# First feed-forward product: the third pair's first four block products ahead of the last ones of the first two pairs, and the sums of the first results spread over later products

## The chip, the cores and the metric

The kernel runs on one core of one Trainium2 chip, in one launch. The metric is the time of an execution on the device in microseconds (us).

## The reference

A decoder block on x (1, 1024, 1024), float32: two token mixers side by side, a gated merge, then a feed-forward part, with adaptive norms in front of both and a norm at the end. The change lies in the first product of the feed-forward part:

```python
h = modulate(rms_norm(x, norm2_g[l]), sh2, sc2)
x = x + g2[:, None, :] * squared_relu_mlp(h, w_ff1[l], w_ff2[l])

def squared_relu_mlp(h, w1, w2):
    return jnp.square(jax.nn.relu(h @ w1)) @ w2     # w1 1024 x 4096, w2 4096 x 1024
```

## The kernel before

Everything is transposed: features lie on the 128 partitions, the 1024 tokens on the free axis. Every float32 operand of a matmul is split into a high half (rounded by ScalarE, a cast) and a low half (VectorE, the operand less the high half), and each product is three matmuls: low times high, high times low, high times high (`mm3`, lines 219, 221, 223).

**Pairs and seven products.** The first feed-forward product makes 4096 hidden features in 16 *pairs* of 128-feature tiles, pair 0 to pair 15 (the first pair is pair 0). Each pair is computed by a Strassen-like scheme: weights and activations are cut into 2 x 2 blocks, and seven block products replace eight. Their names, in the order of a pair, are `ORDER = ("11", "s1", "s3", "s2", "12", "22", "s4")`. A product is twelve matmuls of 128 x 128 by 128 x 512: four slices of the inner dimension by the three of `mm3`. (2,"s3") below means product "s3" of pair 2.

Products work on operands made from the activations: "11" and "12" on blocks of the activations, "s1", "s2", "s3" and "22" on sums of blocks (t1, t2, t3, t4), "s4" on a block. On the weights' side "s1" to "s4" use sums of weight blocks: a running sum that each of the "s" products of a pair takes on from the one before ("s3" has a buffer half of its own).

**PSUM banks.** Each pair has four banks, and some products share one: "11" and "12" bank 0 (called a), "s1" and "s4" bank 1 (d), "s2" bank 2 (b), "s3" and "22" bank 3 (c). The second product of a bank adds to what the first one left.

**The class `Blocks`** records the work of a pair:

- `prep` makes the weights of a product ready: for an "s" product VectorE adds two blocks (line 261); ScalarE casts the high half (line 266). The low half (line 276) is put off until the next `prep`, or `flush`, so that VectorE need not wait for the cast at once.
- `mm` records the twelve matmuls.
- `post` works on the results. After "11" ScalarE copies a (line 298). After "s2" VectorE does the combining: u less b (line 309), then v = c less u (line 310), then the output of "22" from v and d (line 2220). After "12", "22" and "s4" three more outputs follow. The first two pairs use another form, in which d is copied out of PSUM first (lines 302, 305, 306).
- Each output goes through relu and square on ScalarE (lines 2221, 2222 or 2218, 2222) and is stored by a DMA of SP's queue (lines 2228, 2230).
- `run` walks a list of products. For each it calls `before` (loads), records the matmuls, prepares the weights of later products as slots come free, does `post` and calls `after`.

**Slots.** Prepared weights live in 18 slots. Some of them (one tag for a first use, later the ring of six tiles `wh` and `wl` and two of the pool `att`) are used again, so that `run` prepares about as many products ahead as it has finished.

**Sums for the second product.** The second feed-forward product needs sums of blocks of the hidden activations. `a_sums(q, 0)` makes two of them (lines 2237, 2238), `a_sums(q, 1)` two more (lines 2241, 2242), each pair of sums in one tile, stored by one DMA (line 2244).

**The order of work.** Nothing is reordered behind the program: each engine runs its instructions in the order in which they were recorded, and waits on semaphores. `ff1` writes the beginning out by hand: the products of pairs 0 and 1 alternate, while VectorE and ScalarE still make the operands t1 to t4 out of the second half of the tokens. Then `run` takes over with the rest, beginning with

```python
items = sums[:2] + [(0, "22"), (1, "22")] + sums[2:]
late = {(0, "22"): (0, 0), (1, "22"): (1, 0), (2, "s2"): (0, 1), (2, "12"): (1, 1)}
```

so that the order on TensorE is (2,"11"), (2,"s1"), (0,"22"), (1,"22"), (2,"s3"), (2,"s2"), (2,"12"), (2,"22"), (2,"s4"), (3,"11") and so on. `late` says after which product which sums are made.

**Weights from HBM.** `w1_load(q, part)` loads the two halves of a pair's weights on SP's queue (line 2194): pair 2 into the ring `raw` of three tiles, from pair 3 on into the ring `g0` of eight, which also holds the outputs. SP's queue works in order too: a load behind a store waits until that store's data are ready.

Of the kernel before, what the change touches and what calls it, by code (L numbers as in the profile page):

```python
# [133 lines left out]
def block_kernel(ctx, tc, io, stop=None, dbg=None):  # L134
# [240 lines left out]
    def rstd_rows(acc, name, pool, meanwhile=None):  # L375


        nb = acc.shape[1] // P
        ss = ps_s(name + "ss")
        for b in range(nb):  # L380
            nc.tensor.matmul(ss[:, b:b + 1], acc[:, b * P:(b + 1) * P], ones, start=True, stop=True)
        if meanwhile:
            meanwhile()
        return rstd_of(ss[:, :nb], name, pool)
# [8 lines left out]
    def rstd_bcast(rs, b0, nb, name):  # L393

        rb = ps_s(name + "rb")
        for b in range(nb):
            nc.tensor.matmul(rb[:, b * P:(b + 1) * P], rs[:, b0 + b:b0 + b + 1].to_broadcast([P, P]),
                             ident, start=True, stop=True)
        return rb[:, :nb * P]
# [1701 lines left out]
    def x1_load(f, src=None):  # L2101

        t = G["p"].tile([P, S], F32, tag="g0", bufs=8, name=f"x1{'r' if src else ''}_{f}")
        nc.sync.dma_start(t, (src or io["xT"])[f])
        G["x1", f] = t
# [77 lines left out]
    NS = 3  # L2183
    a_d = {t: dram.tile([P, S], F32, name=f"ad{t}") for t in range(8 * NS, 2 * NQ)}
    xs_d = [dram.tile([P, 7, 4, 512], F32, name=f"xsd{c}") for c in range(NS)]
    def w1_load(q, part):

        if q < 2:
            t = G["p"].tile([P, 1024], F32, tag="g1", bufs=8, name=f"w1r{q}{part}")
        elif q < 3:  # L2190
            t = wraw.tile([P, 1024], F32, tag="raw", name=f"w1r{q}{part}")
        else:
            t = G["p"].tile([P, 1024], F32, tag="g0", bufs=8, name=f"w1r{q}{part}")
        nc.sync.dma_start(t, io["w_ff1"][2 * q + part - 1])
        BF.raw[q, part] = t
# [36 lines left out]
    def a_sums(q, part):  # L2232

        e, o = M["out", q]
        r = A["r1"].tile([P, 2, 512], F32, tag="att", bufs=8, name=f"as{q}{part}")
        if part == 0:
            nc.vector.tensor_sub(r[:, 0], e[:, :512], e[:, 512:])
            nc.vector.scalar_tensor_tensor(r[:, 1], r[:, 0], -1.0, o[:, 512:], op0=ALU.mult, op1=ALU.subtract)
            M["t2", q] = r[:, 1]
        else:  # L2240
            nc.vector.tensor_sub(r[:, 0], o[:, 512:], e[:, 512:])
            nc.vector.scalar_tensor_tensor(r[:, 1], M.pop(("t2", q)), -1.0, o[:, :512], op0=ALU.mult,
                                           op1=ALU.subtract)
        nc.sync.dma_start(xs_d[q // 4][:, 3 + 2 * part:5 + 2 * part, q % 4], r)

    BF = Blocks("f", X, ["g1"] * 4 + ["att*"] * 4 + ["att"] * 2 + ["att*"] * 2 + ["wh", "wl"] * 3,
                lambda kind: kind in ("att", "wh", "wl"), f_place, f_sums, f_temps, f_out)

    def x_split(name, m, src, pool, tag, bufs, k=None):

        if tag == "mh":
            hi, lo = mh(f"x{name}{m}h"), mh(f"x{name}{m}l")
        else:
            t = pool.tile([P, 1024], F32R, tag=tag, bufs=bufs, name=f"x{name}{m}")
            hi, lo = t[:, :512], t[:, 512:]
        X[name, m] = hi, lo
        if k is None:
            nc.scalar.copy(hi, src)
            return lambda: nc.vector.tensor_sub(lo, src, fv(hi))
        sh = mods[:, SH2 + k:SH2 + k + 1]  # L2260
        nc.scalar.activation(hi, src, AF.Identity, bias=sh)
        return lambda: nc.vector.scalar_tensor_tensor(lo, src, sh, fv(hi), op0=ALU.add, op1=ALU.subtract)

    def ff1(ahead):
        def t_(k, half):
            return G["x1", k][:, 512 * half:512 * half + 512]

        def norm(k):
            t = t_(k, 1)
            nc.vector.scalar_tensor_tensor(t, t, a2[:, k:k + 1], G["rb"], op0=ALU.mult, op1=ALU.mult)  # L2270


        BF.mm(0, "11", range(3))
        G["rs"] = rstd_rows(G["acc", "n21"], "n21", G["mp"], lambda: BF.prep((2, "11"), (2, "s1")))
        BF.mm(0, "11", range(3, 4))
        BF.post(0, "11")
        BF.mm(1, "11", range(2))
        G["rb"] = rstd_bcast(G["rs"], 0, 4, "n21")
        BF.mm(1, "11", range(2, 4))
        BF.post(1, "11")  # L2280
        BF.prep((2, "s3"))
        BF.mm(0, "12")
        BF.mm(1, "12")
        low = None
        for m in range(4):
            norm(2 * m)
            t1 = t_(2 * m, 0)
            nc.vector.tensor_sub(t1, t1, t_(2 * m, 1))
            if low:
                low()  # L2290
            low = x_split("t1", m, t1, None, "mh", 32)
        norm(1)
        low()
        BF.mm(0, "s1")
        BF.mm(1, "s1")
        for m in range(4):
            if m > 0:
                norm(2 * m + 1)
                low()
            low = x_split("22", m, t_(2 * m + 1, 1), None, "mh", 32, 2 * m + 1)  # L2300
            if m % 2 == 0:
                BF.post(m // 2, "s1")
        for m in range(4):
            t3 = t_(2 * m, 1)
            nc.vector.scalar_tensor_tensor(t3, t3, dsh[:, m:m + 1], t_(2 * m + 1, 1), op0=ALU.add, op1=ALU.subtract)
            low()
            if m == 0:
                BF.mm(0, "s4")
                BF.mm(1, "s4")
            low = x_split("t3", m, t3, G["p"], "g1", 8)  # L2310
        for m in range(4):
            k = 2 * m + 1
            t = t_(k, 1)
            nc.vector.scalar_tensor_tensor(t, t, mods[:, SH2 + k:SH2 + k + 1], t_(2 * m, 0), op0=ALU.add, op1=ALU.add)
            low()
            if m == 0:
                BF.mm(0, "s3")
                BF.mm(1, "s3")
            low = x_split("t2", m, t, G["p"], "g1", 8)

        def t4(m):
            k = 2 * m + 1
            t = t_(k, 0)
            nc.vector.scalar_tensor_tensor(t, t, mods[:, SH2 + k:SH2 + k + 1], t_(k, 1), op0=ALU.add, op1=ALU.subtract)
            return x_split("t4", m, t, A["r1"], "att", 8)

        l = t4(0)
        low()
        BF.mm(0, "s2")
        BF.mm(1, "s2")  # L2330
        BF.post(0, "s2")
        l()
        low = t4(1)
        l = t4(2)
        low()
        BF.post(0, "12")
        BF.post(1, "s2")
        l()
        low = t4(3)
        BF.post(0, "s4")  # L2340
        low()
        BF.post(1, "12")
        BF.post(1, "s4")
        for k in range(NK):
            del G["x1", k]
        for part in (1, 2):
            w1_load(3, part)
        sums = [(q, n) for q in range(2, NQ) for n in ORDER]
        items = sums[:2] + [(0, "22"), (1, "22")] + sums[2:]

        def before(q, n):
            if (q, n) == (2, "22"):
                for part in (1, 2):
                    w1_load(4, part)
            if q > 2 and n == ORDER[0] and q + 2 < NQ:
                for part in (1, 2):
                    w1_load(q + 2, part)
            if q == NQ - 1 and n in ("s2", "12"):
                for f in range(3):
                    x1_load(f + 3 * (n == "12"), x1_d)  # L2360

        late = {(0, "22"): (0, 0), (1, "22"): (1, 0), (2, "s2"): (0, 1), (2, "12"): (1, 1)}
        late.update({(q + 1, n): (q, part) for q in range(2, 4 * NS) for part, n in enumerate(("11", "s1"))})

        def after(q, n):
            if (q, n) in late:
                a_sums(*late[q, n])
            if q == NQ - 2 and n in ("12", "22"):
                b_raw(0, "11", int(n == "22"))
            if q == NQ - 1:  # L2370
                second_ahead(n)

        BF.run(items, sums[3:], before, after, ("s2",))
        x1_load(6, x1_d)
        x1_load(7, x1_d)
        b_x(1, 0)
        b_x(1, 1)
# [17 lines left out]
    def b_raw(c, b, s):  # L2395

        tag = RAWS[c][b].split()[s]
        pool = {"raw": wraw, "rl": G["mp"]}.get(tag, whl)
        t = pool.tile([P, 1024], F32, tag=tag, bufs=2 if tag == "rl" else 3, name=f"w2r{c}{b}{s}")
        nc.sync.dma_start(t, io["w_ff2s"][(4 * c + ("11", "12", "21", "22").index(b)) * 2 + s])  # L2400
        B[c, b, s] = t
# [213 lines left out]

    nff = DFF // P
    steps.add(ff1, manual=True)
    steps.add(ff2_blocks, manual=True)
    behind = []
# [146 lines left out]
```

## Time and profile before

| | us |
|---|---|
| three runs | 2184.2, 2184.3, 2186.07 |
| median | 2184.3 |
| the profiled execution | 2182.82 |
| its span, first to last instruction | 2181.1 |
| 1.7 us lie around the span | |

The mean granted clock of TensorE in the profiled execution is 0.998 of full speed. The first feed-forward product runs from 1534 us to 1849 us of the span.

How to read the views: PE is TensorE (matmuls), PEld its weight loads, DVE VectorE, ACT ScalarE, SP the engine whose queue issues the DMAs. A row of a timeline has start, duration, engine, source line, operation, output<-inputs, shape; in brackets the idle time in front of it and what ended it. A matmul's row lasts 0.39 us, but matmuls overlap: one starts every 0.23 us. A row of the waits has the waiting engine, tile and line, the one waited for, the total in us, how many times, the longest. A row of the stretches has its bounds, its length, then for PE, PEld, DVE, ACT and POOL busy time and (instructions), then TensorE's granted clock, the DMA engines' busy share, and GB/s.

### The profile page before, as it was taken

The page shows a single profiled execution, that of the slowest core. Times are in us where ns is not written, and L with a number is a line of the kernel's source. Part 1 is how long each engine was busy: PE and PEld are TensorE (multiplying, and loading weights), DVE is VectorE, ACT ScalarE, POOL GpSimd, SP SyncE. Part 2 cuts the span into 40 slices and gives each one's busy share as a digit, 9 for nine tenths or more (in the row PEclk, how much of TensorE's full clock was granted, in tenths as well). Part 3 has the DMA queues.
Part 4 walks back from the last instruction along what each step waited for, and adds up shares of the span by engine and source line. Part 5 has one row for each costly group of instructions (what it writes and reads, how often), then busy time and mean ns, then how long its engine had stood idle before and what let it go on. Part 6 is the DMA issues. An engine that isn't in the chain of part 4 may idle for free.

```text
span 2181.1 us, 27045 instructions
## 1 busy us (share of the span) xinstructions
PE 2147.4 (98%) x10034; PEld 1784.6 (82%) x10034; DVE 1479.0 (68%) x2281; ACT 947.1 (43%) x1715; POOL 178.4 (8%) x192
## 2 busy tenths in 40 slices
PE   7999999999999999999999999999999999999998
PEld 5888888888888888888888888888878888788887
DVE  6756777767566678854655644677876665887855
ACT  4533322333334566654644525434554455433412
POOL 0101111100000334410000000001000000000003
PEclk9999999999999999999999999999999999999999
DMA  9869998734687758977323366653054445645322
GB/s 382 231 193 297 289 328 266 217 136 155 223 297 287 257 181 242 263 222 186 105 81 108 98 250 210 224 184 130 35 202 159 154 143 188 240 138 173 109 87 78
DMA packets 161891, 422.55 MB, mean 194 GB/s; under 512 B 27734, under 2 KB 55645, under 8 KB 157662
## 3 DMA queue, kind: packets, MB, share of 16 engines
q1 hardware_dynamic: 151902, 372.57, 48.4%
q0 software_dynamic: 9856, 48.24, 10.1%
q8 instruction: 79, 1.29, 0.2%
q14 instruction: 54, 0.44, 0.1%
HBM read 325.71 MB, written 160.32 MB: 223 GB/s over the span
## 4 chain that ended last, share of the span: by engine, by line
PE 90%; DVE 4%; ACT 2%; DMA 1%; issue 1%; POOL 0%; SPq 0%; POOLq 0%; DVEq 0%; ACTq 0%
PE qap L219 6%; PE qap L223 6%; PE qap L221 6%; PE fp L219 4%; PE fp L223 4%; PE fp L221 4%; PE ak L219 2%; PE ak L221 2%; PE ak L223 2%; PE f2a L221 2%; PE f2a L223 2%; PE f2a L219 2%; PE rg L221 1%; PE rg L219 1%; PE rg L223 1%; PE va L221 1%
## 5 line engine op out<-in xcount | busy, mean ns | idle before, releaser
L219 PE MATMUL qap<-hh,qaw 128*128 128x512 f32 x264 | 102.8, 389 | 0.1
L221 PE MATMUL qap<-hl,qaw 128*128 128x512 f32 x264 | 102.7, 389 | 0.0
L223 PE MATMUL qap<-hh,qaw 128*128 128x512 f32 x264 | 102.7, 389 | 0.0
L656 POOL TENSOR_TENSOR j<-qk,j 128x512 fp32r<-128x512 f32 x32 | 48.3, 1513 | 311.7 <-ACT j L655 311.7
L2117 POOL TENSOR_TENSOR accnf<-accnf,sqnf 128x256 f32<-128x256 f32 (+1 forms) x18 | 16.6, 921 | 613.2 <-ACT sqnf L2116 613.2
L2221 ACT ACTIVATE a<-a 128x512 f32<-128x512 f32 x48 | 30.3, 632 | 78.0 <-DVE a L2220 78.0
L219 PEld LDWEIGHTS qap<-hh,qaw 128*128 128x128 f32 x264 | 49.6, 188 | 10.8 <-DVE qat L310 0.5
L221 PEld LDWEIGHTS qap<-hl,qaw 128*128 128x128 f32 x264 | 49.5, 188 | 10.3
L223 PEld LDWEIGHTS qap<-hh,qaw 128*128 128x128 f32 x264 | 49.6, 188 | 10.3
L2410 ACT CAST w2h<-w2s 128x512 fp32r<-128x512 f32 x36 | 22.4, 621 | 78.2 <-DVE w2s L2448 78.2
L2117 POOL TENSOR_TENSOR accn<-accn,sqn 128x512 f32<-128x512 f32 x12 | 15.5, 1294 | 496.0 <-ACT sqn L2116 496.0
L276 DVE TENSOR_TENSOR fw<-w1r,fw 128x512 fp32r<-128x512 f32 x48 | 32.9, 688 | 33.2 <-ACT fw L266 33.2
L1531 ACT ACTIVATE P<-P,ng 128x128 f32<-128x128 f32 (+1 forms) x96 | 41.9, 438 | 29.5 <-DVE ng L1528 29.5
L276 DVE TENSOR_TENSOR qaw<-wa,qaw 128x512 fp32r<-128x512 f32 x66 | 45.0, 686 | 11.1 <-ACT qaw L266 11.1
L1309 DVE SCALAR_TENSOR_TENSOR cossin<-cossin,cb 128x1024 f32<-128x1024 f32 x32 | 39.0, 1220 | 16.4 <-DMA cossin<-in_w_ada_dram 16.4
L219 PE MATMUL fp<-h2h,fw 128*128 128x512 f32 x128 | 50.0, 390 | 0.0
L1955 DVE TENSOR_TENSOR rwl<-rwl,rwh 128x1024 fp32r<-128x1024 f32 x25 | 30.2, 1221 | 29.0 <-ACT rwh L1985 29.0
L221 PE MATMUL fp<-h2l,fw 128*128 128x512 f32 x128 | 49.8, 389 | 0.0
L223 PE MATMUL fp<-h2h,fw 128*128 128x512 f32 x128 | 49.8, 389 | 0.0
L219 PE MATMUL roa<-rh,rwl 128*128 128x512 f32 x128 | 49.8, 389 | 0.0
L221 PE MATMUL roa<-rl,rwh 128*128 128x512 f32 x128 | 49.8, 389 | 0.0
L223 PE MATMUL roa<-rh,rwh 128*128 128x512 f32 x128 | 49.8, 389 | 0.0
(3093 smaller groups left out, 7138.1 us busy)
## 6 DMA issues: line engine op xcount, KB each, us to landing
cossin<-in_w_ada_dram SPq DMA_DIRECT2D x32, 512.0 KB, 5.3
v<-vd SPq DMA_DIRECT2D x32, 512.0 KB, 5.7
w1r<-in_w_ff_dram SPq DMA_DIRECT2D x32, 512.0 KB, 4.8
vd<-vo SPq DMA_DIRECT2D x24, 512.0 KB, 6.3
xsd<-as SPq DMA_DIRECT2D x24, 512.0 KB, 2.8
w2r<-in_w_ff2s_dram SPq DMA_DIRECT2D x24, 512.0 KB, 7.6
em<-in_w_ada_dram SPq DMA_DIRECT2D x16, 512.0 KB, 10.2
wrvs<-in_w_rv_dram POOLq DMA_DIRECT2D x16, 512.0 KB, 11.1
```

Source lines behind the costliest of these rows:

```text
L219: nc.tensor.matmul(o, wl, xh, start=first, stop=False, skip_group_check=skip)
L221: nc.tensor.matmul(o, wh, xl, start=False, stop=False, skip_group_check=skip)
L223: nc.tensor.matmul(o, wh, xh, start=False, stop=last, skip_group_check=skip)
L276: nc.vector.tensor_sub(t[:, 512:], src, fv(t[:, :512]))
L656: nc.gpsimd.tensor_sub(t[:, 1], src, fv(t[:, 0]))
L1309: nc.vector.scalar_tensor_tensor(t, t, 1.0, cb, op0=ALU.mult, op1=ALU.mult, accum_out=mods[:, j:j + 1])
L1531: nc.scalar.activation(v, v, AF.Exp, bias=ng[:, blk:blk + 1], accum_out=st[:, g, blk, 2 + a:3 + a])
L1955: nc.vector.tensor_sub(lo, fv(lo), fv(hi))
L2117: (nc.vector if f == 7 else nc.gpsimd).tensor_add(G["acc", key], G["acc", key], sq)
L2221: nc.scalar.activation(o, o, AF.Relu)
L2410: nc.scalar.copy(hi, src)
```

## The change

Three things are moved; no arithmetic is added or removed, and every engine has as many instructions as before.

1. The weights of (2,"s2") are prepared in the hand-written beginning, between the outputs of (1,"s2") and the last operands, and (2,"s3") and (2,"s2") run ahead of (0,"22") and (1,"22"). The order on TensorE is (2,"11"), (2,"s1"), (2,"s3"), (2,"s2"), (0,"22"), (1,"22"), (2,"12"), (2,"22"), (2,"s4"), (3,"11").
2. `a_sums` of pairs 0, 1 and 2 stand behind later products: (0,0) behind (2,"12"), (0,1) behind (2,"22"), (1,0) behind (2,"s4"), (1,1) behind (3,"11"), (2,0) behind (3,"s1"), (2,1) behind (3,"12").
3. Pair 4's weights are loaded before (2,"12") rather than before (2,"22"), and into the ring `raw` like pair 2's.

```diff
-        elif q < 3:
+        elif q in (2, 4):
             t = wraw.tile([P, 1024], F32, tag="raw", name=f"w1r{q}{part}")
...
         BF.post(0, "12")
         BF.post(1, "s2")
+        BF.prep((2, "s2"))
         l()
         low = t4(3)
         BF.post(0, "s4")
...
-        items = sums[:2] + [(0, "22"), (1, "22")] + sums[2:]
+        items = sums[:4] + [(0, "22"), (1, "22")] + sums[4:]
 
         def before(q, n):
-            if (q, n) == (2, "22"):
+            if (q, n) == (2, "12"):
                 for part in (1, 2):
                     w1_load(4, part)
...
-        late = {(0, "22"): (0, 0), (1, "22"): (1, 0), (2, "s2"): (0, 1), (2, "12"): (1, 1)}
-        late.update({(q + 1, n): (q, part) for q in range(2, 4 * NS) for part, n in enumerate(("11", "s1"))})
+        late = {(2, "12"): (0, 0), (2, "22"): (0, 1), (2, "s4"): (1, 0), (3, "11"): (1, 1),
+                (3, "s1"): (2, 0), (3, "12"): (2, 1)}
+        late.update({(q + 1, n): (q, part) for q in range(3, 4 * NS) for part, n in enumerate(("11", "s1"))})
...
-        BF.run(items, sums[3:], before, after, ("s2",))
+        BF.run(items, sums[4:], before, after, ("s2",))
```

## The prediction

> **What bounds the kernel now.** I read the page first, then the list of waits, the timelines of TensorE, VectorE and ScalarE around the change, and busy time by stretch.
>
> ```profile
> span 2181.1 us, 27045 instructions
> ...
> PE 2147.4 (98%) x10034; PEld 1784.6 (82%) x10034; DVE 1479.0 (68%) x2281; ACT 947.1 (43%) x1715; POOL 178.4 (8%) x192
> ...
> PE 90%; DVE 4%; ACT 2%; DMA 1%; issue 1%; POOL 0%; SPq 0%; POOLq 0%; DVEq 0%; ACTq 0%
> ```
>
> TensorE (PE) is busy for 98% of the span and holds 90% of the chain that ended last. The change keeps every matmul, so it can only gain where TensorE stands still, and it loses wherever it makes TensorE stand still. The list of waits has two of this stage:
>
> ```profile
> PE fp L219 <- DVE ft2nacc L310: 3.3, 1, 3.3
> ...
> PE fp L219 <- DVE ft15h2t L310: 0.8, 1, 0.8
> ```
>
> Both are one mechanism. Products "s3" and "22" of a pair share a PSUM bank. The combining step after "s2" (L309, then L310) reads that bank, so "22" may not add to it before L310 has ended. In the third pair L310 comes 3.3 us late. Rows of TensorE (start, duration; one of the twelve matmuls of a product each, the first one but for the last row):
>
> ```profile
> 1575.97 0.39 PE L219 MATMUL fp<-xt,fw 128*128 128x512 f32 x1
> ...
> 1578.69 0.39 PE L219 MATMUL fp<-xt,fw 128*128 128x512 f32 x1
> ...
> 1586.85 0.39 PE L219 MATMUL fp<-h2h,fw 128*128 128x512 f32 x1
> ...
> 1593.02 0.50 PE L219 MATMUL fp<-xt,fw 128*128 128x512 f32 x1 [3.29 <-DVE ft2nacc L310]
> ...
> 1597.39 0.48 PE L219 MATMUL fp<-x220h,fw2s 128*128 128x512 f32 x1
> ...
> 1600.25 0.39 PE L219 MATMUL fp<-h2h,fw 128*128 128x512 f32 x1
> ...
> 1843.32 0.50 PE L219 MATMUL fp<-xt,fw 128*128 128x512 f32 x1 [0.83 <-DVE ft15h2t L310]
> ...
> 1846.19 0.39 PE L219 MATMUL fp<-x220h,fw15s 128*128 128x512 f32 x1
> ```
>
> (0,"22") starts at 1575.97 and (1,"22") at 1578.69, so a product takes 2.72 us. (2,"12") starts at 1586.85; (2,"22") was due at 1589.57 and starts at 1593.02: 3.45 us lost from start to start. It then takes 4.37 us to 1597.39 in place of 2.72 (1.65 more), and "s4" 2.86 to 1600.25 (0.14 more). The wait costs 5.24 us in all, of which 1.79 come after it. The stretches say why (last columns: granted clock, DMA share, GB/s):
>
> ```profile
> 1593.02:1597.39 4.37, 4.37 (x13) 3.39 (x13) 3.71 (x7) 3.41 (x6) 0.00 (x0) 0.63 0.40 148
> ...
> 1600.20:1619.25 19.05, 19.05 (x85) 15.78 (x85) 13.53 (x22) 9.61 (x17) 0.00 (x0) 1.00 0.64 234
> ...
> 1843.30:1846.20 2.90, 2.88 (x13) 2.37 (x14) 2.09 (x3) 2.12 (x4) 0.00 (x0) 1.00 1.03 411
> ```
>
> The granted clock is 0.63 behind the wait of 3.29 us and 1.00 behind that of 0.83 us, where the product takes 2.87 us (0.15 more).
>
> **The change, part by part.** TensorE now runs (2,"s3") and (2,"s2") in the places of (0,"22") and (1,"22"), at 1575.97 and 1578.69, and the two "22" after them. Whether a wait is left is decided on VectorE, which works in order; its instructions must be followed one by one. These rows give their prices:
>
> ```profile
> 1573.91 0.69 DVE L2220 TENSOR_TENSOR a<-fp,ft1h2t 128x512 f32<-128x512 f32 x1
> ...
> 1575.12 0.75 DVE L2324 SCALAR_TENSOR_TENSOR x<-x,mods 128x512 f32<-128x512 f32 x1
> ...
> 1576.61 0.69 DVE L2259 TENSOR_TENSOR xt<-x,xt 128x512 fp32r<-128x512 f32 x1
> ...
> 1582.49 0.69 DVE L261 TENSOR_TENSOR fs<-fs,w1r 128x512 f32<-128x512 f32 x1
> 1583.86 0.69 DVE L276 TENSOR_TENSOR fw2s<-fs,fw2s 128x512 fp32r<-128x512 f32 x1 [0.69 <-ACT fw2s L266]
> ...
> 1591.56 0.68 DVE L309 TENSOR_TENSOR ft2nacc<-ft2nacc,fp 128x512 f32<-128x512 f32 x1
> 1592.27 0.69 DVE L310 TENSOR_TENSOR ft2nacc<-fp,ft2nacc 128x512 f32<-128x512 f32 x1
> 1593.00 0.69 DVE L2220 TENSOR_TENSOR a<-ft2nacc,fp 128x512 f32<-128x512 f32 x1
> ...
> 1602.33 0.69 DVE L276 TENSOR_TENSOR fw3s<-fs,fw3s 128x512 fp32r<-128x512 f32 x1 [1.27 <-ACT fw3s L266]
> 1602.94 0.68 DVE L2220 TENSOR_TENSOR a<-ft2nacc,fp 128x512 f32<-128x512 f32 x1
> 1605.49 0.69 DVE L276 TENSOR_TENSOR fw<-w1r,fw 128x512 fp32r<-128x512 f32 x1 [1.87 <-ACT fw L266]
> 1606.11 0.68 DVE L2237 TENSOR_TENSOR as<-a 128x512 f32<-128x512 f32 x1
> 1606.82 0.69 DVE L2238 SCALAR_TENSOR_TENSOR as<-as,a 128x512 f32<-128x512 f32 x1
> ...
> 1611.33 0.69 DVE L309 TENSOR_TENSOR ft3nsq<-ft3nsq,fp 128x512 f32<-128x512 f32 x1
> ```
>
> Start to start: 0.61 us for one instruction behind another (1602.33 to 1602.94), 0.71 to 0.73 where it uses the one before (L309, L310, L2220; L2237, L2238). A sum of weight blocks costs 1.37 us from the sum (L261) to its low half (L276), with ScalarE's rounding between (1582.49 to 1583.86). From an output (L2220) to the first low half whose rounding stands behind that output's relu and square on ScalarE it is 2.55 us (1602.94 to 1605.49), and up to two other instructions fit into that. I carry these prices through the changed order.
>
> *Step 1, the start.* The sum for (2,"s2") and the low half for (2,"s3") are put behind L2220 of 1573.91, in front of the last two low halves of the operand t4 (L2259). So: 1574.52 sum, 1575.12 low half of "s3" (ends by 1575.81, needed at 1575.97: just in time), 1575.73 t4's third low half, 1576.33 the last t4 sum (L2324). That step comes 1.21 us later than in its row, so its low half is at 1577.82 (1576.61 − 1575.12 = 1.49 after it), the output of (1,"s4") at 1578.43, the low half for (2,"s2") at 1579.03. It ends 0.69 later, and TensorE starts 0.06 behind that (1592.27 + 0.69 = 1592.96 against 1593.02): 1579.78. Due was 1578.69: **a new wait of 1.09 us**. It lies nearer to the 0.83 us wait than to the 3.29 us one, so I give it full clock and 0.15 us behind it: 1.24 us.
>
> *Step 2, the third pair.* The next low half, for (2,"12"), waits for ScalarE:
>
> ```profile
> 1575.96 0.62 ACT L2258 CAST xt<-x 128x512 fp32r<-128x512 f32 x1
> ...
> 1580.04 0.60 ACT L266 CAST fw2s<-fs 128x512 fp32r<-128x512 f32 x1
> ```
>
> Six relu, square and copy instructions stand between these two casts, 4.08 us start to start. They stand between t4's last cast, now at 1577.12 (behind the sum's end, 1576.33 + 0.75), and the cast for (2,"12") in the new order: 1581.20, done 1581.80. VectorE goes on at 1581.84: low halves 1581.84 and 1582.45, sum for "s4" 1583.05, its low half 1584.42, then L309 at 1585.03, L310 1585.74, output 1586.47. (2,"22") is due on TensorE six places behind (2,"s3"), past 1592; L310 has ended by 1586.43. **The 3.3 us wait goes**, with five microseconds to spare.
>
> *Step 3, the fourth pair: what is late next.* TensorE runs six products from 1579.78 to the end of (2,"s4"): 16.32 + 0.15, so (3,"11") starts at 1596.25 (1600.25 before), and five products later, at 1609.85, (3,"22") is due. VectorE, from 1586.47: low half for (3,"s1") 1589.02; sum for (3,"s3") 1589.63, low half 1591.00; output of (0,"22") 1591.60, low half of (3,"s2") 1594.15; output of (1,"22") 1594.76, low half for (3,"12") 1597.31; first half of the put-off sums of pair 0 1597.92 and 1598.63; low half 1599.24; output 1599.84; second half of pair 0 1600.45 and 1601.05; sum and low half for (3,"s4") 1601.66 and 1603.03; output 1603.63; the first sums of pair 1 inside the 2.55 behind it, low half for (4,"11") 1606.18; second sums of pair 1 1606.79 and 1607.39; sum and low half for (4,"s1") 1608.00 and 1609.37; first sums of pair 2 1609.97 and 1610.68; sum for (4,"s3") 1611.29; and only then L309 at 1611.89, L310 at 1612.60. It ends at 1613.29, and (3,"22") starts at 1613.35. **The wait is back, one pair later: 3.50 us** (before, L309 stood at 1611.33 and was early enough because TensorE itself was 4 us later). VectorE has nearly the same work in front of this L309 as before; the change moves the outputs and sums of the first two pairs behind the third pair's combining step, where they queue before the fourth's.
>
> *Step 4, the clock.* A gap of 3.50 is as long as one of 3.45 that was followed by clock 0.63; I price its tail the same: 1.65 + 0.14. A bound from below is the 0.15 behind the 0.83 us wait.
>
> *Step 5, loads and stores.* Median landing times in this stretch:
>
> ```profile
> w1r<-in_w_ff_dram SPq DMA_DIRECT2D x8, 512.0 KB, 4.6
> xsd<-as SPq DMA_DIRECT2D x8, 512.0 KB, 3.4
> ```
>
> The fifth pair's weights go into another ring and are asked for before (2,"12"). On SP's queue they stand behind the store of (1,"22"): output 1594.76, relu, square, so about 1596.8, landed by about 1602, first cast behind the output of 1603.63: nothing, with over 2 us of cover. The put-off sums have two buffers; each pair of sums waits for the store of the last but one. The tight one: pair 1's first sums end by 1605.6, stored by about 1609.4; pair 2's first sums take the buffer at 1609.97. I take 0, with 0.5 us of cover.
>
> *The sum.* Removed: 3.45 + 1.65 + 0.14 = 5.24. Added: 1.24 at (2,"s2") and 3.50 + 1.79 = 5.29 at (3,"22"), 6.53. Net **+1.3 us**. Behind the fourth pair TensorE has no other wait until the 0.83 us one and all is shifted alike. The profiled execution took 2182.82 us (span 2181.1), so it would take 2184.1; against the median of the three runs, 2184.3, I forecast **2185.6 us**. About 0.2%, 4.4 us, is what a measurement of this kernel can tell from no change.
>
> **Rivals.**
>
> *The slow clock does not follow the moved wait.* For it: one case of it is all the trace has. Then the tail is 0.15 in place of 1.79, net −0.3: 2184.0. [...] Chance 0.11.
>
> *Faster: VectorE reaches the fourth pair's L309 in time.* ScalarE holds up VectorE for some 10 us in my steps 2 and 3; if its casts come earlier than in the rows I used, 3.5 us could be caught up. Then only the 1.24 us is added: −4.0, 2180.3; without that too −5.2, 2179.1. Against it: each price is a repeated row of the same instructions. Chance 0.17.
>
> *Slower: the put-off sums stall VectorE on their stores.* Two 512 KB loads of the sixth pair stand right behind the store of pair 1's first sums. Each microsecond beyond the 0.5 of cover lengthens the wait at (3,"22") by as much. Past 0.2% it needs 3.1 us more, a landing near 7 us; then 2188.7 and up, with a lengthened slow stretch (another 1.65) about 2190. For: the DMA share is 0.64 there already. Against: the 3.4 us median. Chance 0.24.
>
> The forecast keeps 0.48.
>
> **How the numbers follow.** The likeliest gives 2185.6; its own range, from prices that are off by 0.1 us over some 40 steps, is 2184 to 2188. 2180.2 to 2189.5 takes in the first rival, the nearer half of the faster one and over half of the slower one, and leaves out less than 2 in 10. Faster by over 0.2%: two thirds of the faster rival, 0.12. Slower by over 0.2%: most of the slower one, 0.22. Within: 0.66.
>
> **What would show it.** Right: the list of waits has no third-pair wait of TensorE on L310, a wait of about 1.1 us on VectorE at (2,"s2") near 1579.8, and one of about 3.5 us on the fourth pair's L310, with a clock near 0.63 behind it; (3,"11") starts near 1596.3 and (4,"11") near 1620.6 (before 1600.25 + 7 × 2.72 = 1619.3). Wrong: no wait on the fourth pair's L310, or VectorE waiting for a store of the sums.

## The result and the profile after

| | before | changed |
|---|---|---|
| median of 20 runs each, us | 2184.29 | 2187.55 |
| the profiled execution: span, us | 2181.1 | 2186.0 |
| ratio changed to before, 95% interval | | 1.0015 [1.0009, 1.0022] |

3.3 us slower, inside the 0.2% that the prediction called no change, above the 2185.6 us forecast. The loss is small, but its interval lies above 1. Out of the list of waits of the changed kernel, in order of their totals, what TensorE (PE) waited for in this stage and what VectorE (DVE) waited for on stores (waiting engine, tile and line; total, times, longest):

```profile
PE fp L219 <- DVE ft3h2t L310: 5.4, 1, 5.4
...
DVE as L2237 <- DMA xsd<-as: 1.8, 1, 1.8
...
PE fp L219 <- DVE fw2s L276: 0.9, 1, 0.9
DVE as L2241 <- DMA xsd<-as: 0.5, 1, 0.5
```

The third pair's wait on L310 (3.3 us) is gone. In its place stand 0.9 us at (2,"s2") and 5.4 us one pair later, and VectorE waits for stores of the sums, which it did nowhere in this stage before. TensorE's timeline (first matmuls of (2,"s1"), (2,"s3"), (2,"s2"), (3,"11"), (3,"22"), (3,"s4"), (4,"11")):

```profile
1574.30 0.50 PE L219 MATMUL fp<-xt10h,fw2s 128*128 128x512 f32 x1
...
1577.20 0.40 PE L219 MATMUL fp<-xt,fw2s 128*128 128x512 f32 x1
...
1580.97 0.50 PE L219 MATMUL fp<-xt,fw2s 128*128 128x512 f32 x1 [0.87 <-DVE fw2s L276]
...
1597.46 0.39 PE L219 MATMUL fp<-h2h,fw 128*128 128x512 f32 x1
...
1616.60 0.80 PE L219 MATMUL fp<-xt,fw 128*128 128x512 f32 x1 [5.38 <-DVE ft3h2t L310]
...
1621.80 0.39 PE L219 MATMUL fp<-x220h,fw3s 128*128 128x512 f32 x1
...
1624.56 0.39 PE L219 MATMUL fp<-h2h,fw 128*128 128x512 f32 x1
```

The same two ends before:

```profile
1573.09 0.50 PE L219 MATMUL fp<-xt10h,fw2s 128*128 128x512 f32 x1
...
1619.29 0.39 PE L219 MATMUL fp<-h2h,fw 128*128 128x512 f32 x1
```

From the third pair's "s1" to the fifth pair's "11" it was 46.20 us and is 50.26: **4.06 us longer, and this is the change.** (Fifteen products of 2.72 us are 40.8.) The rest of the 4.9 us between the two spans lies outside this stretch: 1.21 us had been lost before it, where TensorE has the same work in both kernels, 1.14 us are won between (4,"11") and the second product, most of it the 0.83 us wait of pair 15, which this execution did not have (of the nine traces here only those of the kernel before and of third_buf have it), and 0.77 us are lost after that. VectorE's timeline of the changed kernel at the fourth pair shows where its time went:

```profile
1587.00 0.69 DVE L310 TENSOR_TENSOR ft2nacc<-fp,ft2nacc 128x512 f32<-128x512 f32 x1
...
1605.03 0.68 DVE L2220 TENSOR_TENSOR a<-ft2nacc,fp 128x512 f32<-128x512 f32 x1
1607.53 0.69 DVE L2237 TENSOR_TENSOR as<-a 128x512 f32<-128x512 f32 x1 [1.82 <-DMA xsd<-as]
...
1610.02 0.69 DVE L2241 TENSOR_TENSOR as<-a,a 128x512 f32<-128x512 f32 x1 [0.46 <-DMA xsd<-as]
...
1615.14 0.68 DVE L309 TENSOR_TENSOR ft3nsq<-ft3nsq,fp 128x512 f32<-128x512 f32 x1
1615.85 0.69 DVE L310 TENSOR_TENSOR ft3h2t<-fp,ft3nsq 128x512 f32<-128x512 f32 x1
```

The first sums of pair 1 (L2237) and its second sums (L2241) stand still until a buffer's store has landed, and the fourth pair's L309 stands behind both. On SP's queue the late store is plain to see:

```profile
1598.56 1.34 SPq L2194 DMA_DIRECT2D w1r<-in_w_ff_dram  x2
1600.70 0.38 SPq L2244 DMA_DIRECT2D xsd<-as  x1
```

The store of pair 0's first sums is issued at 1600.70, right behind two 512 KB loads, and VectorE gets its buffer at 1607.53, 6.8 us later. The busy times of the changed kernel in the stretch behind the wait (last columns: clock, DMA share, GB/s):

```profile
1616.60:1621.80 5.20, 5.20 (x13) 4.11 (x13) 4.54 (x8) 3.92 (x7) 0.00 (x0) 0.51 0.27 104
```

### The profile page after: what moved, and what is told of

The parts are those of the page before. It is cut to its first block, busy times and chain, and to the rows that moved or that the text cites. A ratio compares the mean times of both kernels' runs of the same rounds, so it can differ in the third digit from the quotient of the medians.

```text
span 2186.0 us, 27043 instructions
## 1 busy us (share of the span) xinstructions
PE 2149.2 (98%) x10034; PEld 1785.4 (82%) x10034; DVE 1478.8 (68%) x2281; ACT 947.1 (43%) x1715; POOL 178.6 (8%) x192
## 3 DMA queue, kind: packets, MB, share of 16 engines
q8 instruction: 79, 1.29, 0.2%
## 4 chain that ended last, share of the span: by engine, by line
PE 90%; DVE 4%; ACT 2%; DMA 2%; issue 1%; POOL 0%; POOLq 0%; DVEq 0%; SPq 0%; ACTq 0%
PE qap L219 6%; PE qap L223 6%; PE qap L221 6%; PE fp L219 4%; PE fp L221 4%; PE fp L223 4%; PE ak L219 2%; PE f2a L221 2%; PE f2a L223 2%; PE f2a L219 2%; PE ak L221 2%; PE ak L223 2%; PE rg L221 1%; PE rg L219 1%; PE rg L223 1%; PE va L221 1%
## 5 line engine op out<-in xcount | busy, mean ns | idle before, releaser
L266 ACT CAST qaw<-wa 128x512 fp32r<-128x512 f32 x66 | 39.7, 617 | 23.5 <-PE qap L223 15.2
```

Source lines behind the costliest of these rows:

```text
L266: nc.scalar.copy(t[:, :512], src)
```

## The experiments

**Theory A:** the time is set by VectorE's queue in front of each pair's L309. The new order of products brings TensorE to the fourth pair's "22" earlier than VectorE can be done; the put-off sums add waits for their stores. **Theory B:** the order of products is right, and the putting off alone is the loss. **Theory C:** VectorE's work can only be moved, so what is spared in one pair is paid in the next.

Kernels of the first four experiments were compared with 29 runs of the kernel before on their chip (median 2182.83 us), the last three with 27 (2182.97). "Stage" is from (2,"s1") to (4,"11") in the profile; the waits are TensorE's, the last column VectorE's on stores.

| kernel | median us | ratio to before, 95% interval | stage us | at (2,"s2") | 3rd pair's L310 | 4th pair's L310 | stores |
|---|---|---|---|---|---|---|---|
| before | 2184.29 | 1 | 46.20 | – | 3.3 | – | – |
| changed | 2187.55 | 1.0015 [1.0009, 1.0022] | 50.26 | 0.9 | – | 5.4 | 2.3 |
| order_only | 2186.89 | 1.0021 [1.0012, 1.0030] | 49.79 | 0.9 | – | 4.3 | 0.6 |
| sums_only | 2185.28 | 1.0009 [1.0000, 1.0018] | 47.01 | – | 1.2 | 2.9 | 2.9 |
| third_buf | 2185.05 | 1.0009 [1.0000, 1.0017] | 48.67 | 0.9 | – | 3.5 | – |
| load_later | 2188.70 | 1.0030 [1.0019, 1.0041] | 50.87 | 0.9 | – | 6.3 | 2.6 |
| old_buf | 2178.95 | 0.9981 [0.9972, 0.9990] | 42.57 | – | 1.2 | – | – |
| old_buf4 | 2179.50 | 0.9984 [0.9975, 0.9992] | 42.41 | – | 1.2 | – | – |
| free_buf | 2180.62 | 0.9990 [0.9981, 0.9999] | 43.76 | 0.9 | – | 1.3 | – |

**order_only: the new order, the sums as early as it allows.** Against the changed kernel:

```diff
-        late = {(2, "12"): (0, 0), (2, "22"): (0, 1), (2, "s4"): (1, 0), (3, "11"): (1, 1),
-                (3, "s1"): (2, 0), (3, "12"): (2, 1)}
-        late.update({... for q in range(3, 4 * NS) ...})
+        late = {(0, "22"): (0, 0), (1, "22"): (1, 0), (2, "12"): (0, 1), (2, "22"): (1, 1)}
+        late.update({... for q in range(2, 4 * NS) ...})
```

> The new order of products, but the sums of pairs 0 to 2 made as early as that order allows: (0,0) behind (0,"22"), (1,0) behind (1,"22"), (0,1) behind (2,"12"), (1,1) behind (2,"22"), pair 2's behind (3,"11") and (3,"s1") as in the kernel before. Theory A (the order of products alone brings TensorE to the fourth pair's "22" earlier than VectorE can be done; the putting off is no cause of it): the wait of about 0.9 us at (2,"s2") stays, the wait on the fourth pair's L310 is 3 to 4 us, VectorE waits for no store; 2 us slower than the kernel before, about 2186.3. Theory B (the putting off and its stores are the loss): the fourth pair's wait is below 1 us and the kernel is 2 to 4 us faster than before, about 2181.5.

Measured: 4.1 us slower than before, and 4.3 us of wait at the fourth pair; in front of it VectorE waits 0.6 us for a store, which theory A had not expected. The order alone moves the wait and makes it longer. Theory B falls.

**sums_only: the old order, the sums put off.** Against the kernel before, `late` alone is the changed kernel's.

> The old order of products and loads, with the sums put off as in the changed kernel. Theory A: four VectorE instructions (2.6 us) leave the queue in front of the third pair's L309, so TensorE's wait there falls from 3.3 us to 1 to 1.5 us and no longer lowers the clock; the fourth pair's wait is 0 to 2 us, depending on how late the stores are; 1.5 to 3.5 us faster than the kernel before, about 2182. Theory B: VectorE waits about 2 us for stores as in the changed kernel, the wait moves to the fourth pair with 2 us or more and a lowered clock, and nothing is gained: 2183.5 to 2186.

Measured: the third pair's wait falls to 1.2 us as theory A has it, but the loss by stores is at the upper end of its range and beyond: one wait of 2.9 us, and a wait of 2.9 us at the fourth pair. VectorE's timeline of this kernel:

```profile
1606.91 0.69 DVE L2241 TENSOR_TENSOR as<-a,a 128x512 f32<-128x512 f32 x1 [2.92 <-DMA xsd<-as]
```

The median is 2.4 us above before; the profiled execution, at 2183.22 us, was among the shortest of the eleven. On this kernel theory B's numbers, not A's, came out: with two buffers, putting off brings no gain in either order.

**third_buf: the changed kernel with one more buffer.**

```diff
-        r = A["r1"].tile([P, 2, 512], F32, tag="att", bufs=8, name=f"as{q}{part}")
+        r = (wraw.tile([P, 2, 512], F32, tag="raw", name=f"as{q}{part}") if (q, part) == (1, 0)
+             else A["r1"].tile([P, 2, 512], F32, tag="att", bufs=8, name=f"as{q}{part}"))
```

> The changed kernel with a third buffer for the put-off sums: pair 1's first sums go into the free tile of the ring raw. Theory A: the 2.3 us that VectorE waits for stores go (below 0.5 us), the fourth pair's wait falls from 5.4 us to 3 to 3.5 us, 2.3 us faster than the changed kernel, about 2185.3, still no faster than the kernel before. Theory B: the fourth pair's wait falls below 1 us and the kernel is faster than before.

Measured as theory A said: no wait on a store, and on TensorE's timeline of this kernel the fourth pair's wait is

```profile
1614.32 0.79 PE L219 MATMUL fp<-xt,fw 128*128 128x512 f32 x1 [3.55 <-DVE ft3h2t L310]
```

The wait is 3.55 us. From start to start 3.71 us are lost ((3,"12") starts at 1607.89, so (3,"22") was due at 1610.61); the prediction's queue, with no store late, had given 3.50. So of the changed kernel's 5.4 us about 1.8 are stores, and the 3.5 left are VectorE's queue under the new order: old_buf, below, has the sums as late and no such wait. The stage is 1.6 us shorter than the changed kernel's, not the 2.3 expected, because the time lost behind the wait did not fall with it (2.79 us against 2.52).

**load_later: the loads of pair 4 behind that store.**

```diff
-            if (q, n) == (2, "12"):
+            if (q, n) == (2, "22"):
```

> The changed kernel with pair 4's weights loaded before (2,"22") again, so behind the store of pair 0's first sums on SP's queue and not in front of it. If that store is late because 1 MB of loads stands right in front of it, VectorE's wait of 1.8 us for it falls below 0.5 us, the fourth pair's wait falls from 5.4 us to 3.5 us, and it is about 2 us faster than the changed kernel, 2185.5. If it is late because of the stores of the outputs behind and before it, the wait stays above 1.3 us and the time at 2187 to 2188.

Measured: neither. VectorE no longer waits for pair 0's first store, but 2.6 us for its second one, which now stands behind the same loads (VectorE's timeline of this kernel):

```profile
1610.16 0.69 DVE L2241 TENSOR_TENSOR as<-a,a 128x512 f32<-128x512 f32 x1 [2.63 <-DMA xsd<-as]
```

From 1602 to 1608 its DMA engines are full, as the windows' last two columns say (DMA share, GB/s):

```profile
1602.00:1608.00 6.00, 6.00 (x28) 4.92 (x28) 4.21 (x7) 3.35 (x6) 0.00 (x0) 1.00 1.01 319
```

In both kernels the store behind the megabyte of loads is the late one: VectorE waited 1.82 us for it in the changed kernel and 2.63 us here. What helped was a buffer that does not wait for it (third_buf).

**old_buf: the old order, the sums put off, three more buffers.** Against the kernel before, the changed `late`, and the tiles of (0,1), (1,0), (1,1) from the ring `raw` as in third_buf (pair 4's weights stay in `g0`, so all three tiles of `raw` are free by then).

> The old order of products with the sums put off as in the changed kernel, and three tiles of the ring raw as further buffers for (0,1), (1,0) and (1,1), so that no sum waits for a store. Theory A (VectorE's queue in front of L309, lengthened by waits for stores, is all of it): third pair's wait 1.2 us at full clock as in the experiment with the sums alone, no VectorE wait on a store, fourth pair's wait at most 0.5 us; from the third pair's "s1" to the fifth's "11" about 42.5 us (46.2 before); 3 to 4 us faster than the kernel before. Theory C (putting sums off only moves VectorE's work, so the fourth pair must pay whatever is spared in the third): the fourth pair's wait stays at 2 to 3 us with a lowered clock, no gain.

Measured as theory A said: 4.0 us faster than the kernel before. One wait is left on TensorE's timeline of this kernel:

```profile
1591.94 0.50 PE L219 MATMUL fp<-xt,fw 128*128 128x512 f32 x1 [1.17 <-DVE ft2nacc L310]
```

The busy times of that kernel in the stretch behind it (last columns: clock, DMA share, GB/s) show that the clock stays at 1.00:

```profile
1591.94:1594.80 2.86, 2.85 (x13) 2.36 (x13) 2.19 (x4) 2.12 (x4) 0.00 (x0) 1.00 0.49 183
```

VectorE's timeline of the same kernel: it reaches the fourth pair's L309 right behind its last sum:

```profile
1609.08 0.69 DVE L261 TENSOR_TENSOR fs<-w1r,w1r 128x512 f32<-128x512 f32 x1
1609.68 0.68 DVE L309 TENSOR_TENSOR ft3nsq<-ft3nsq,fp 128x512 f32<-128x512 f32 x1
```

The same sums stand in front of it as in the changed kernel, and TensorE does not wait. Theory C falls: what the third pair spares, the fourth need not pay.

**old_buf4: the same, the sums further apart.** `late = {(2, "12"): (0, 0), (2, "s4"): (0, 1), (3, "11"): (1, 0), (3, "s1"): (1, 1), (3, "12"): (2, 0), (3, "s4"): (2, 1)}`.

> As the kernel with the old order and three more buffers, but the sums further apart: (0,0) behind (2,"12"), (0,1) behind (2,"s4"), (1,0) behind (3,"11"), (1,1) behind (3,"s1"), (2,0) behind (3,"12"), (2,1) behind (3,"s4"). Theory A: third pair's wait 1.2 us, fourth's none, about 42.3 us from the third pair's "s1" to the fifth's "11", 3.5 to 4 us faster than the kernel before. Theory C: a wait of 1.5 us or more in the fourth or fifth pair.

Measured: 3.5 us faster than before, stage 42.41 us; not to be told apart from old_buf.

**free_buf: the changed kernel's order, the sums behind the fourth pair's combining.** `late = {(2, "s4"): (0, 0), (3, "11"): (0, 1), (3, "12"): (1, 0), (3, "22"): (1, 1), (3, "s4"): (2, 0), (4, "11"): (2, 1)}`, later pairs' behind the next pair's "s1" and "s4", and the buffer of third_buf.

> The changed kernel's order of products, with the sums put behind the fourth pair's combining where they can be: (0,0) behind (2,"s4"), (0,1) behind (3,"11"), (1,0) behind (3,"12"), (1,1) behind (3,"22"), (2,0) behind (3,"s4"), (2,1) behind (4,"11"), later pairs' behind the next pair's "s1" and "s4"; one more buffer. Theory A: six VectorE instructions (3.6 us) and the store waits leave the queue in front of the fourth pair's L309: wait at (2,"s2") 0.9 us, at the fourth pair 1.5 to 2 us, in the fifth at most 0.5 us; 44 to 45 us from the third pair's "s1" to the fifth's "11"; 1 to 2 us faster than the kernel before, 4 to 5 us faster than the changed one. Theory C: the wait moves on to the fifth pair with 2 us or more and the kernel is no faster than the one before.

Measured: 2.3 us faster than before, with the two waits that theory A names (0.9 and 1.3 us, the second shorter than it said, and the gain larger) and none in the fifth pair. So the new order can gain if VectorE's queue in front of the fourth L309 is cut, but it keeps its own wait of 0.9 us; the old order with the same care is better.

The best version is old_buf, at 0.9981 [0.9972, 0.9990] of the kernel before: the second part of the change without the first, with buffers for it. The third part, pair 4's earlier loads into the ring `raw`, was not run alone: load_later takes back their time, not their ring.

## Why the prediction was right, and where its size was off

The direction of the sum, its range and "within 0.2%" held; the forecast was 1.3 us up, the runs gave 3.3 and the profile's stage 4.06. By its steps (the profiled execution ran 1.20 us later at the start of this stretch: L306 of pair 1 at 1574.39 against 1573.19):

- *Step 1, the wait at (2,"s2").* 1.09 us were due; (2,"s2") was due at 1577.20 + 2.72 = 1579.92 and started at 1580.97: 1.05. Right.
- *Step 2, the third pair.* L310 at 1585.74 + 1.20 = 1586.94; measured 1587.00. Right, and the 3.3 us wait is gone. ("Past 1592" for (2,"22") counts one product too many: it stands five places behind (2,"s3"), so it was due at 1590.81, and at 1592.02 it started 1.21 us after that, the shift of this execution. The cover was 4.4 us rather than five, and nothing hung on it.)
- *Step 3, the fourth pair.* (3,"11") at 1596.25 + 1.20 = 1597.45; measured 1597.46. L309 at 1611.89 + 1.20 = 1613.09; measured 1615.14, 2.05 late. (3,"22") was due at 1597.46 + 13.6 = 1611.06 and started at 1616.60: 5.54 us lost in place of 3.50. VectorE waits 1.82 + 0.46 = 2.28 us for stores in front of it, part of it in place of a wait for ScalarE. Without late stores (third_buf) L309 came at 1612.86 against 1611.89 + 0.78 = 1612.67, 0.19 us late, and 3.71 us were lost: the step's own number came out to 0.2 us, and the stores are the other 1.9.
- *Step 5, loads and stores,* is **the step that failed**: it gave nothing for the sums' buffers. It took the median landing of 3.4 us. Only two of those eight stores are timed in the trace before (3.5 us, issued at 1599.28, and 3.2 us, at 1610.73), and no load was issued in the 5 us before either. The same trace had the case that mattered: a 512 KB store of an output (L2230), issued at 1601.81 right behind two loads, took 5.5 us, another one at 1587.11, with no load near, 2.8 us. And the step looked at the wrong buffer: the tight one was not pair 2's first sums but pair 1's, whose buffer pair 0's store still held. It cost about 1.9 us in L309, and the rival that names this mechanism priced it rightly one to one, if with the wrong store.
- *Step 4, the clock.* 1.79 us were given for the time lost behind the wait. Measured: "22" 5.20 us and "s4" 2.76, against 2.72 each, 2.52 lost. Off by 0.7: the clock was low for 6.83 us here, for 3.41 us before (last section).

So the net of 1.3, the 2.04 by which 5.54 exceeds 3.50, and 0.73 of clock give 4.07 against 4.06 in the profile. One of the two signs that the prediction had named as showing it wrong did come: VectorE waited for stores of the sums. Its path, VectorE's queue up to the fourth pair's L309, was right but not complete; that the time still fell between 2184 and 2188 us, its own range, is luck in so far as no term of the sum covered that wait. The slow clock did follow the moved wait: 0.51 behind 5.38 us in the changed kernel, 0.50 behind 4.34 us in order_only and 3.55 us in third_buf, 0.52 behind 2.93 us in sums_only, so that rival fell; the faster rival fell too, since VectorE ran by the rows' prices, to 0.2 us at the fourth L309 where no store was late. The slower rival's mechanism was there, but at 1.9 us it stayed below the point that the rival needed for 0.2%.

## What to carry to other kernels

Work that comes earlier on the bounding engine only helps if what feeds it can keep up at the next such point too: follow the in-order queue of the feeding engine, instruction by instruction, past the wait that goes to the one after it (here 3.3 us went at the third pair and 5.4 us came at the fourth). Work that is put off needs buffers for as long as it is put off: with two buffers the gain went into waits for stores (2.9 us in sums_only), with three more it came out (4.0 us in old_buf). The landing time of stores with no load close in front says little about a store behind a megabyte of loads: in the trace before 2.8 to 3.5 us without such loads, 5.5 us behind them.

## What the runs showed of the hardware that was not expected

**The clock fell behind a shorter gap than 3.3 us, and stayed low for 3.41 us or for 6.83.** After waits of 0.87, 1.17 and 1.29 us the granted clock stayed at 1.00; after 2.93 us it fell. The busy times of sums_only in the stretch behind that wait:

```profile
1613.49:1616.70 3.21, 3.21 (x8) 2.58 (x9) 2.55 (x5) 2.48 (x5) 0.00 (x0) 0.52 0.10 38
```

And those of free_buf in the stretch behind 1.29 us:

```profile
1613.87:1616.74 2.87, 2.87 (x13) 2.37 (x14) 2.20 (x4) 2.14 (x4) 0.00 (x0) 1.00 0.32 125
```

Time lost on the two products behind the wait, over 2 × 2.72 us: 0.14 us behind 1.29 us; 1.52 behind 2.93; 1.79 behind 3.29; 2.79 behind 3.55; 2.63 behind 4.34; 2.52 behind 5.38; 2.18 behind 6.35. It does not grow with the gap. The clock in the traces goes with these numbers. In the kernel before it stood at one half for 3.41 us (1594.17 to 1597.59), in the changed one for 6.83 us (1614.86 to 1621.69); in order_only it was 0.50 over the 5.30 us from 1615.20 on, in third_buf over the 5.58 us from 1614.32 on. About half of the slow time still left when the wait ended was lost. The busy times of the changed kernel, cut where the clock changes:

```profile
1614.86:1621.68 6.82, 5.08 (x12) 4.03 (x13) 6.09 (x11) 4.54 (x8) 0.00 (x0) 0.50 0.47 182
1621.70:1630.00 8.30, 8.30 (x37) 6.82 (x37) 5.12 (x9) 4.03 (x7) 0.00 (x0) 1.00 0.74 267
```

TensorE went on at 1616.60, 5.09 us before the clock rose, and lost 2.52. In load_later, by an estimate from its matmuls' rows (0.63 us each up to 1620.32, 0.39 us from 1621.14 on), 4.4 us were left (2.18 lost); in sums_only, by an estimate from the 0.52 over 3.21 us above, 3.1 us (1.52 lost).

The clock also fell where TensorE had stood still for less. In third_buf it fell once more, at 1865.78 in the second product:

```profile
1862.37:1865.77 3.40, 1.68 (x7) 0.86 (x6) 1.79 (x3) 2.09 (x2) 0.00 (x0) 1.00 0.99 400
1865.79:1869.19 3.40, 3.40 (x9) 2.65 (x9) 2.36 (x4) 0.62 (x1) 0.00 (x0) 0.50 0.67 220
```

TensorE had stood still for 1.7 us of the 3.40 us in front of that fall (3.40 − 1.68), and for 2.3 us of the 3.41 us in front of the fall in the kernel before.

In the traces of the kernel before and of the changed one, all changes of the clock lie whole multiples of 3.413 us apart. Before: up at 24.04 us of the span, down at 1594.17, up at 1597.59, down at 2174.44, which is 460, 1 and 169 times 3.413 us. Changed: 24.25, 1614.86, 1621.69, 2178.06, which is 466, 2 and 163 times. Counted in stretches of that length on that grid, from 30 us of the span on, TensorE stood still for 2.26 and 2.22 us (before) and 3.41 and 2.42 us (changed) of the stretches that ended with a fall, and for at most 1.04 us of every other stretch at full clock. As the ends of matmuls are modelled, these are estimates. What makes the clock fall no run tried by itself.

**A store behind loads.** Issued behind two 512 KB loads on one queue, a 512 KB store of the changed kernel freed its buffer after 6.8 us, twice the median landing of 3.4 us before, and moving the loads past it only made the next store late (VectorE waited 2.6 us for it in load_later). Whether it is the queue's order or the engines' bandwidth (share 1.01 from 1602 to 1608 in load_later) was not told apart.
